# A hybrid decoder layer on one core: matrix factors finished in an earlier pass, retention re-stepped with one root per head, sums of weights written sooner

## The chip, the core and the metric

The kernel runs on one core of a Trainium2 chip. A core has a matrix engine (TensorE, PE in the profile; its weight loads are listed apart as PEld), a vector engine (VectorE, DVE), a scalar engine (ScalarE, ACT), GpSimd (POOL) and a queue processor that here issues nearly all transfers (SyncE, SP). Each engine works through its own list of instructions in order and waits for others by semaphores. The metric is the time of one launch in microseconds (us) of device time.

## The reference, cut to what matters

All is float32: 1024 tokens, model width 2048, 16 heads of width 128, eight of them stick-breaking attention and eight retention.

```python
mod = silu(c) @ w_ada + b_ada
shift, scale, gate = split(mod, 3)
h = rms_norm(x, norm_gain) * (1 + scale) + shift          # 1024 x 2048
proj = h @ w_in                                           # 2048 x 8192
q_sb, k_sb, v_sb, z_sb, q_r, k_r, v_r, z_r = split(proj)  # 1024 columns each
oa = stick_breaking(rms(q_sb), rms(k_sb), v_sb) * silu(z_sb)
o_t = sum_{s<=t} gamma_h^(t-s) (rot(q_t) . rot(k_s)) v_s  # retention, in chunks of 128 tokens:
      # scores within a chunk times a decay mask, plus q times a state carried over the chunks
ob = (o - mean) * rsqrt(var + eps) * gain * silu(z_r)     # mean and variance per head and token
out = x + gate * (concat(oa, ob) @ w_out)
```

## The kernel before, in words

**Precision.** A float32 product is made of three matmuls in the faster fp32r format (`mm3`): each operand is cut into a high half (a rounding copy on ACT) and a low half (operand minus high half, on DVE): high x high, high x low, low x high. `split` does this for a 128x512 tile of weights and takes its buffers from a ring of four.

**The input projection by seven products.** The normalised input, transposed, is a 2x2 arrangement of blocks B11, B12, B21, B22 (eight tiles of 128x512 each, one for each `k` from 0 to 7), the weights of a column pair a 2x2 arrangement A11 to A22. Instead of eight block products the kernel makes seven, in the manner of Strassen and Winograd. Their right-hand factors are B11, B21, B22 and the combinations T1 to T4 (`RIGHT`); for every `k` each must be formed and cut into halves. Their left-hand factors are blocks of weights or sums of them, each cut by `split`. Columns are taken in seven groups: four for stick-breaking (q, k, z, v of two heads each), two for retention's k and v, the last for retention's z. Group 0 goes through the products in the order `ORDER1` = 2 (B21), 7 (T3), 4 (T4), 1 (B11), 6 (T2), 5 (T1), 3 (B22), the others in `ORDER` = 4, 1, 6, 5, 3, 2, 7. An entry is one product for 512 contraction rows and one column block: 12 matmuls of 512 columns (`run_entry`). The left operand of an entry is prepared three entries ahead (`LOOK`).

**Before group 0.** Loads of x, its normalisation, and the modulation from `w_ada` run beside a first projection of seven retention q heads (`start_mm`), done in two passes over the 16 contraction blocks: one for the first 512 tokens, one for the last 512. In the second pass each of the 16 positions has seven heads; after each head, items are taken from two lists. `urgent` holds the whole blocks B21, B12, B22, B11 (scale and shift on ACT) and the halves of B21, `background` the forming of T3 and its halves. After positions 3, 7, 11 and 15 `factors` adds the items of two more `k`. A third list, `late`, holds all of T1, T2, T4, B22 and B11; it is appended to `background` after the second pass and taken off two items at every `tick`, which comes twice an entry, in group 0. Factors of B21, T3, T4 and B11 stay in SBUF until group 0 has used them and are then stored; T1, T2 and B22 are stored at once. Later groups read all factors back through a ring.

**Buffers and queues.** SBUF holds 92 slots of 128x512 float32 that `Slots` hands out, from group 0's 24th entry on by classes: 14 for results, 24 raw weights, 24 ring, 30 attention. A slot given back is used again only once its last reader or its store is done. PE's order is written out by hand; attention runs as generators that `tick` moves on, at most one step a tick, each asking for so many ticks until its next step. `later(n, fn)` puts off a piece of ACT or DVE work by `n` ticks.

**Sums of weights.** In group 0, product 7 needs A11 - A21 and product 3 of every group A12 - A11. Both subtractions are issued in `left`, directly ahead of the split that reads them.

**Stick-breaking.** `prepare(h)` loads q and k, forms the norms' roots, stores a row of key scales and loads it back broadcast (`back`). `sb_attention(h)` begins when that is ready and the head before is far enough: it loads q again and v, splits k, and three ticks later splits q.

**Retention.** `ret_prepare` loads a head's q, k, v and rotates q and k on DVE. `ret_attention` takes nine steps on PE, `gap` ticks apart (3, and 2 from head 5 on; 2 ticks ahead of the first): transpose k of chunks 0 to 3 (`turn_k(0)`), transpose v (`values_in(0)`), states 0 with `turn_k(1)`, `values_in(1)` with scores 0, states 1, values 0, scores 1, values 1, and the turning back of the result (`finish`), whose second half is put off into the next head. One tick after scores DVE multiplies them by the mask (`pT`) and POOL scales q; one tick after states DVE makes the chain of states; one tick after values comes `norm`: four statistics and four aggregates on DVE, a root of ten small instructions (`rsqrt_newton`), and four ACT instructions that read the PSUM bank. The four PSUM banks A0, A1, B, C are used in turn. Retention begins when the last stick-breaking head is done and group 5 has begun; the preparation of head 4 waits for group 6.

**Output projection.** It follows in four column units, the first split in two halves of tokens.

Of the kernel before, what the change touches and what calls it, by code (L numbers as in the profile page):

```python
# [17 lines left out]
P = 128  # L18
S = 1024
D = 2048  # L20
KC = D // P
# [12 lines left out]
RT_GAP2 = 2  # L34
# [18 lines left out]
class Slots:  # L53
# [3 lines left out]
    def __init__(self, pool, n):  # L57
        self.pool, self.of, self.cls, self.need = pool, {}, {}, {}
        self.free = {None: deque(range(n))}

# [17 lines left out]
    def get(self, name, cls=None, dtype=F32, borrow=False):  # L78
        q = self.free.get(cls) or self.free[None]
        if not q and borrow:  # L80
# [18 lines left out]
def layer_kernel(ctx, tc, x, c, w_ada, b_ada, norm_gain, w_in, sb_q_gain, sb_k_gain, ret_norm_gain, w_out,  # L99
# [209 lines left out]
    def left(gi, prod, hh, q):  # L309

        def r(b):
            return raws[gi, q, b, hh]

        def done(b):
            put(raws.pop((gi, q, b, hh)))

        name = f"{gi}_{prod}_{q}_{hh}"
        if q == 4:
            b = "A12" if prod in (2, 3) else "A11"
            w = split(r(b), name)  # L320
            if prod in (5, 3):
                done(b)
            return w
        if prod == 7 and gi == 0:
            t = get(f"S3_{q}_{hh}", "raw", borrow=True)
            nc.vector.tensor_tensor(t, r("A11"), r("A21"), op=ALU.subtract)
            sum_done.add((gi, hh, q, 3))
            w = split(t, name)
            put(t)
            return w  # L330
        if prod == 6:
            while (gi, hh, q, 3) not in sum_done or (gi, hh, q, 1) not in sum_done:
                one_sum(*sums1.popleft())
            while (gi, hh, q, 2) not in sum_done:
                one_sum(*sums2.popleft())
        elif prod == 3:
            nc.vector.tensor_tensor(r("A11"), r("A12"), r("A11"), op=ALU.subtract)
# [7 lines left out]
        return w  # L345

# [106 lines left out]
    def run_entry(j):  # L453
        gi, prod, hh, q = entries[j]
        prepare_entry(j + LOOK)
# [133 lines left out]

    def factors(ks):  # L590
# [15 lines left out]
        def high(n, k):  # L606
            def fn():
                t = facs[n, k, "hi"] = get(f"{n}h_{k}", None, F32R, borrow=True)
                nc.scalar.activation(t, facs[n, k], AF.Copy)  # L609
            return fn  # L610

        def low(n, k):
            def fn():
                src, hi = facs[n, k], facs.pop((n, k, "hi"))
                lo = get(f"{n}l_{k}", None, F32R, borrow=True)
                nc.vector.tensor_tensor(lo, src, hi.bitcast(F32), op=ALU.subtract)
                if n != "B21":
                    put(facs.pop((n, k)))
                if n in FIXED:
                    fixed[n, k] = hi, lo  # L620
                else:
                    store(n, k, hi, lo)
                    put(hi, lo)
            return fn

# [142 lines left out]
    for p in range(KC):  # L768
# [11 lines left out]
        for i, h in enumerate((0, 1, 2, 3, 4, 5, 6) if p < KC - 1 else (3, 4, 5, 6, 0, 1, 2)):  # L780
# [9 lines left out]
            some(urgent, 2)  # L790
            if i in (1, 4, 5, 6):
                some(background, 1)
# [8 lines left out]
    background.extend(late)  # L801
    for j in range(LOOK):
        prepare_entry(j)
# [76 lines left out]
    scales, kss = {}, {}  # L880

    def prepare(h):
# [78 lines left out]
    def sb_attention(h, gap):  # L961
# [8 lines left out]
        q_, k_, v_, qt = {}, {}, {}, []  # L970
        for hf in range(2):
            qt.append(get(f"q_{h}_{hf}", "att"))
            nc.sync.dma_start(qt[hf], proj[f"q{h}"][:, halves(hf)])
# [171 lines left out]
    tables, pending, done_concat = {}, [], set()  # L1145
# [35 lines left out]
    def ret_attention(h, r, gap):  # L1181
# [64 lines left out]
        def values(g):  # L1246
# [10 lines left out]
            def norm():  # L1257
                st6 = sm.tile([P, 4, 6], F32, tag="st6", name=f"st6_{h}_{g}")
                mv = sm.tile([P, 4, 2], F32, tag="mv", name=f"mv_{h}_{g}")
                for j in range(4):  # L1260
                    nc.vector.bn_stats(st6[:, j, :], op[:, j, :])
                for j in range(4):
                    nc.vector.bn_aggr(mv[:, j, :], st6[:, j, :])
                m = sm.tile([P, 4], F32, tag="m4", name=f"m4_{h}_{g}")
                nc.vector.tensor_scalar(m, mv[:, :, 1], EPS, None, op0=ALU.add)
                y = sm.tile([P, 4], F32, tag="y4", name=f"y4_{h}_{g}")
                u = sm.tile([P, 4], F32, tag="u4", name=f"u4_{h}_{g}")
                rsqrt_newton(y, m, u)
                nc.vector.scalar_tensor_tensor(u, mv[:, :, 0], -1.0, y, op0=ALU.mult, op1=ALU.mult)
                for j in range(4):  # L1270
                    nc.scalar.activation(on[:, j * P:(j + 1) * P], op[:, j, :], AF.Identity, scale=y[:, j:j + 1],
                                         bias=u[:, j:j + 1])
            later(1, norm)
# [15 lines left out]
        yield 2  # L1289
# [16 lines left out]
        scores(1)  # L1306
# [3 lines left out]
        yield gap  # L1310
        finish(0)
        pending.append(lambda: finish(1))
        yield gap

    def ret_heads():
        while prog.get(NH - 1, 0) < 99 or phase[0] < 5:
            yield 1
# [5 lines left out]
        yield 16  # L1323
        for h in range(NH):
            r = nxt
            for i, wait in enumerate(ret_attention(h, r, RT_GAP if h < 5 else RT_GAP2)):
# [5 lines left out]
        yield 4  # L1332
        pending.pop()()
# [50 lines left out]
    for i in range(8):  # L1384
        load_at[i] = [(b, i // 4, i % 4) for b in ("A11", "A21")]
        load_at[8 + i] = [("A22", i // 4, i % 4)]
    for i in range(2):
        load_at[16 + i] = [("A11", i, 4)]
    for j in range(len(entries)):
        gi, prod, hh, q = entries[j]  # L1390
        if j == 0 or entries[j - 1][0] != gi:
# [5 lines left out]
            if gi == 5:  # L1397
                start(ret_heads(), 3)
            if gi == 1:
# [151 lines left out]
```

## Time and profile before

| | |
|---|---|
| runs of the kernel before | 2032.77 us median of 3 (2032.35 to 2036.83) |
| the profiled execution | 2034.63 us, its span 2032.9 us |
| PE, share of the span | 95% (1939.3 us) |
| DVE | 61% |
| ACT | 39% |
| POOL | 4% |
| mean granted TensorE clock | 0.985 |
| HBM read, written | 410.04 MB, 75.54 MB |

The profile gives, for each engine, its busy time, what ended its idle times (the releaser), single instructions in order of time, and tables of stretches of time. A name such as `pT<-sp,dm` means that tile pT was written from sp and dm, `L1240` is line 1240 of the kernel, and `x64` counts instructions. Where one helper records every split, rows of different callers have the same line and are told apart by the names of tiles.

### The profile page before, as it was taken

The numbers are of one execution on the slowest core, as the hardware profiler recorded it, in microseconds if no ns is written. First come the engines' busy times: TensorE is split into PE (matmuls) and PEld (weight loads), VectorE is DVE, ScalarE is ACT, GpSimd is POOL, SyncE is SP. The second block draws the span as 40 slices with busy tenths as digits, with TensorE's granted clock in tenths as the row PEclk, the third lists the DMA queues.
The fourth block names the chain that finished last, engine by engine and source line by source line (L and its number), as shares of the span: only waits on it lengthen the run. The fifth ranks groups of instructions, "written<-read, shape, count | busy, mean of one in ns | idle before, by whom it ended". The sixth has DMA issues, their size and how long they took to land.

```text
span 2032.9 us, 28401 instructions
## 1 busy us (share of the span) xinstructions
PE 1939.3 (95%) x9703; PEld 1581.2 (78%) x9703; DVE 1245.0 (61%) x2485; ACT 789.2 (39%) x1481; POOL 78.0 (4%) x278
## 2 busy tenths in 40 slices
PE   5999986999999999999999999999989999999998
PEld 4776764787878877888888888887878778788887
DVE  4645567346767666767686767665866667635122
ACT  5446643224544454445444543333333444211110
POOL 0000000000100010001000010000000000000000
PEclk9999997999999999999999999999999999999999
DMA  9966598798788678867877787989959636745041
GB/s 314 360 223 218 192 314 295 248 342 284 233 269 289 224 238 282 277 230 246 286 269 239 251 277 242 287 263 279 338 176 265 209 120 219 239 128 191 21 151 62
DMA packets 381725, 487.51 MB, mean 240 GB/s; under 512 B 30734, under 2 KB 201864, under 8 KB 381580
## 3 DMA queue, kind: packets, MB, share of 16 engines
q1 hardware_dynamic: 381192, 485.65, 73.0%
q8 instruction: 76, 1.25, 0.3%
q14 instruction: 69, 0.57, 0.1%
q10 hardware_dynamic: 388, 0.04, 0.0%
HBM read 410.04 MB, written 75.54 MB: 239 GB/s over the span
## 4 chain that ended last, share of the span: by engine, by line
PE 77%; DMA 8%; DVE 8%; ACT 3%; issue 2%; SPq 1%; ACTq 0%; DVEq 0%
PE pj L185 14%; PE pj L186 14%; PE pj L187 14%; PE y L185 5%; PE y L186 5%; PE y L187 5%; PE first L185 2%; PE first L186 2%; PE first L187 2%; PE accp L553 1%; DMA q<-pr_q 1%; DVE wl L174 1%; ACT wh L172 1%; PE op L1251 1%; PE oT L187 1%
## 5 line engine op out<-in xcount | busy, mean ns | idle before, releaser
L174 DVE TENSOR_TENSOR wl<-A,wh 128x512 fp32r<-128x512 f32 x392 | 270.3, 691 | 311.6 <-ACT wh L172 285.1
L172 ACT ACTIVATE wh<-A 128x512 fp32r<-128x512 f32 x392 | 246.9, 631 | 390.7 <-PE pj L186 292.2
L185 PE MATMUL y<-wh_o,ch 128*128 128x512 f32 x512 | 201.1, 393 | 2.4 <-ACT ch L1378 2.3
L187 PE MATMUL y<-wh_o,cl 128*128 128x512 f32 x512 | 200.3, 391 | 0.0
L186 PE MATMUL y<-wl_o,ch 128*128 128x512 f32 x512 | 200.0, 391 | 0.0
L174 DVE TENSOR_TENSOR wl_o<-wo,wh_o 128x512 fp32r<-128x512 f32 x80 | 54.9, 690 | 173.9 <-ACT wh_o L172 173.1
L172 ACT ACTIVATE wh_o<-wo 128x512 fp32r<-128x512 f32 x80 | 50.4, 630 | 236.1 <-PE y L187 212.1
L380 DVE TENSOR_TENSOR c<-pj,c 128x512 f32<-128x512 f32 x112 | 75.0, 688 | 75.6 <-PE pj L187 75.4
L377 ACT ACTIVATE c<-pj 128x512 f32<-128x512 f32 x112 | 66.5, 598 | 129.4 <-PE pj L187 109.0
L185 PEld LDWEIGHTS y<-wh_o,ch 128*128 128x128 f32 x512 | 96.6, 189 | 24.5 <-ACT ch L1378 3.1
L187 PEld LDWEIGHTS y<-wh_o,cl 128*128 128x128 f32 x512 | 96.5, 188 | 21.3 <-DVE cl L1379 1.1
L186 PEld LDWEIGHTS y<-wl_o,ch 128*128 128x128 f32 x512 | 96.5, 189 | 19.7
L295 DVE TENSOR_TENSOR A<-A,A 128x512 f32<-128x512 f32 x160 | 108.7, 687 | 1.9
L185 PE MATMUL pj<-T4h,wh 128*128 128x512 f32 x224 | 91.7, 410 | 13.5 <-ACT T4h L609 13.5
L185 PE MATMUL pj<-T3h,wh 128*128 128x512 f32 x224 | 90.3, 403 | 5.1 <-ACT wh L172 5.1
L1030 DVE TENSOR_TENSOR_SCAN om<-om 128x128 f32<-128x128 f32 (+2 forms) x96 | 93.7, 976 | 1.1
L185 PE MATMUL first<-h_hi,wh_first 128*128 128x512 f32 x224 | 92.4, 413 | 1.1 <-ACT h_hi L583 1.1
L185 PE MATMUL pj<-B21h,wh 128*128 128x512 f32 x232 | 93.0, 401 | 0.0
L185 PE MATMUL pj<-B22h,wh 128*128 128x512 f32 x232 | 92.8, 400 | 0.0
L185 PE MATMUL pj<-T1h,wh 128*128 128x512 f32 x232 | 92.6, 399 | 0.0
L187 PE MATMUL pj<-T4h,wl 128*128 128x512 f32 x224 | 89.6, 400 | 3.0 <-DVE wl L174 3.0
L185 PE MATMUL pj<-B11h,wh 128*128 128x512 f32 x232 | 91.4, 394 | 0.0
(236 smaller groups left out, 4620.7 us busy)
## 6 DMA issues: line engine op xcount, KB each, us to landing
A<-in_w_in_dram SPq DMA_DIRECT2D x228, 256.0 KB
ada<-in_w_ada_dram SPq DMA_DIRECT2D x128, 256.0 KB
wo<-in_w_out_dram SPq DMA_DIRECT2D x80, 256.0 KB
gr<-in_w_ada_dram SPq DMA_DIRECT2D x64, 256.0 KB
T2h<-fac_T SPq DMA_DIRECT2D x56, 256.0 KB
T2l<-fac_T SPq DMA_DIRECT2D x56, 256.0 KB
T1h<-fac_T SPq DMA_DIRECT2D x56, 256.0 KB
T1l<-fac_T SPq DMA_DIRECT2D x56, 256.0 KB
```

What stands on the lines that cost most here:

```text
L172: nc.scalar.activation(hi[:, 0:n], src[:, 0:n], AF.Copy)
L174: nc.vector.tensor_tensor(lo[:, 0:n], src[:, 0:n], hi[:, 0:n].bitcast(F32), op=ALU.subtract)
L185: nc.tensor.matmul(o, a_hi, b_hi, start=first, stop=False, skip_group_check=on)
L186: nc.tensor.matmul(o, a_hi, b_lo, start=False, stop=False, skip_group_check=on)
L187: nc.tensor.matmul(o, a_lo, b_hi, start=False, stop=last, skip_group_check=on)
L295: nc.vector.tensor_tensor(r[o], r[a], r[b], op=ALU.add if n == 1 else ALU.subtract)
L377: nc.scalar.activation(t, o, AF.Copy)
L380: nc.vector.tensor_tensor(dst[q, cc], o, dst[q, cc], op=ALU.add)
L553: nc.tensor.matmul(ap_[32 * g:32 * g + 32, :], silu_z[:, j, :], ada[cc, j // 2][:, (j % 2) * 256:(j % 2) * 256 + 256], start=j < 4, stop=j ...
L1030: nc.vector.tensor_tensor_scan(rev, rev, rev, init, op0=ALU.mult, op1=ALU.bypass)
L1251: nc.tensor.matmul(op[:, j, :], pT[:, tk], vb(i), start=True, stop=(i == 0))
```

## The change

Factors: after the second pass's positions 3, 7 and 11, all of T1 to T4 and B22 for two `k` goes into `background` and is taken off within that pass; only the last two `k` (`last`) are left over to group 0, with all halves of B11, which come last of all. The taking off is spread otherwise: one urgent item a head (two at the last position), and background items only while six or fewer urgent ones are left, then one or two a head. `high` and `low` move out of `factors` unchanged.

Sums: `prepare_sum` issues the subtractions two entries ahead of their split; group 0's raw blocks A11, A21, A22 are loaded one entry later. In the last group a slot may be taken from any class (`loose`).

Stick-breaking: q is loaded in `prepare`, behind the broadcast row.

Retention: eight steps, 3 ticks apart for all heads, in another order; statistics of both halves are kept and one root is formed for eight chunks; a copy of the result is taken from PSUM by ACT, and the normalisation later works on that copy in SBUF. Both halves of `finish` are put off into the next head. Its tables and the first head's loads begin before the last stick-breaking head ends.

```diff
     def run_entry(j):
         gi, prod, hh, q = entries[j]
+        prepare_sum(j + LOOK + 2)
         prepare_entry(j + LOOK)
...
+    def prepare_sum(j):
+
+        if j >= len(entries):
+            return
+        gi, prod, hh, q = entries[j]
+        if q < 4 and prod == 3:
+            a = raws[gi, q, "A11", hh]
+            nc.vector.tensor_tensor(a, raws[gi, q, "A12", hh], a, op=ALU.subtract)
+        elif gi == 0 and prod == 7:
+            early_sum[hh, q] = t = get(f"S3_{q}_{hh}", "raw", borrow=True)
+            nc.vector.tensor_tensor(t, raws[gi, q, "A11", hh], raws[gi, q, "A21", hh], op=ALU.subtract)
+            sum_done.add((gi, hh, q, 3))
...
+        last = 7 in ks
         for k in ks:
             urgent.extend(whole(n, k) for n in ("B21", "B12", "B22", "B11"))
             urgent.extend((high("B21", k), low("B21", k)))
-            background.extend((minus("T3", "B22", "B12", k), high("T3", k), low("T3", k)))
-            late.extend((over("T1", "B12", "B11", k), minus("T2", "B22", "T1", k), over("T4", "B21", "T2", k)))
-            order = ("T4", "T1", "T2", "B22", "B11")
-            late.append(high("T4", k))
+        for k in ks:
+            background.extend((minus("T3", "B22", "B12", k), high("T3", k), over("T1", "B12", "B11", k), low("T3", k),
+                               minus("T2", "B22", "T1", k), over("T4", "B21", "T2", k), high("T4", k)))
+            order = ("T4", "T2", "T1", "B22")
             for i, n in enumerate(order):
+                q = late if last and i else background
                 if i + 1 < len(order):
-                    late.append(high(order[i + 1], k))
-                late.append(low(n, k))
+                    (late if last else background).append(high(order[i + 1], k))
+                q.append(low(n, k))
...
-            some(urgent, 2)
-            if i in (1, 4, 5, 6):
-                some(background, 1)
+            if len(urgent) <= 6:
+                some(background, 1 if urgent or i % 4 == 3 else 2)
+            some(urgent, 1 if p < KC - 1 else 2)
...
     background.extend(late)
+    background.append(high("B11", 0))
+    for k in range(8):
+        if k < 7:
+            background.append(high("B11", k + 1))
+        background.append(low("B11", k))
...
                 nc.sync.dma_start(kb[hf], krow[h][:, halves(hf)].broadcast_to([P, HALF]))
+            qs[h] = [get(f"q_{h}_{hf}", "att") for hf in range(2)]
+            for hf in range(2):
+                nc.sync.dma_start(qs[h][hf], proj[f"q{h}"][:, halves(hf)])
...
-            def norm():
+            def stats():
+                nc.scalar.activation(on, op.rearrange("p j n -> p (j n)"), AF.Copy)
...
+            later(1, stats)
+            if g:
+                later(2, roots)
...
+            later(3, lambda: norm(0))
+            later(4, lambda: norm(1))
...
-        yield 2
         turn_k(0)
         yield gap
         values_in(0, vr[0])
-        if pending:
-            pending.pop()()
+        scores(0)
+        yield gap
+        turn_k(1)
         yield gap
         states(0)
-        turn_k(1)
+        scores(1)
         yield gap
         values_in(1, vr[1])
-        scores(0)
-        yield gap
-        states(1)
+        if pending:
+            pending.popleft()()
         yield gap
         values(0)
         yield gap
-        scores(1)
+        states(1)
+        if pending:
+            pending.popleft()()
         yield gap
         values(1)
...
-        while prog.get(NH - 1, 0) < 99 or phase[0] < 5:
+        while prog.get(NH - 1, 0) < 12 or phase[0] < 5:
...
-        load_at[i] = [(b, i // 4, i % 4) for b in ("A11", "A21")]
-        load_at[8 + i] = [("A22", i // 4, i % 4)]
+        load_at[i + 1] = [(b, i // 4, i % 4) for b in ("A11", "A21")]
+        load_at[9 + i] = [("A22", i // 4, i % 4)]
```

More of the change, by code (lines that the diff above doesn't have):

```diff
@@ L33 @@
 RT_GAP = 3
-RT_GAP2 = 2
 NZ = 7
@@ L79, in get @@
         q = self.free.get(cls) or self.free[None]
-        if not q and borrow:
+        if not q and (borrow or self.loose):
             q = max(self.free.values(), key=len)
@@ L324, in left @@
         if prod == 7 and gi == 0:
-            t = get(f"S3_{q}_{hh}", "raw", borrow=True)
-            nc.vector.tensor_tensor(t, r("A11"), r("A21"), op=ALU.subtract)
-            sum_done.add((gi, hh, q, 3))
+            t = early_sum.pop((hh, q))
             w = split(t, name)
@@ L335, in left @@
                 one_sum(*sums2.popleft())
-        elif prod == 3:
-            nc.vector.tensor_tensor(r("A11"), r("A12"), r("A11"), op=ALU.subtract)
         b = {1: "A11", 2: "A12", 3: "A11", 4: "A22", 5: "A22", 6: "A11", 7: "A21"}[prod]
@@ L588, in layer_kernel, with high, fn, low @@
     facs = {}
+    def high(n, k):
+        def fn():
+            t = facs[n, k, "hi"] = get(f"{n}h_{k}", None, F32R, borrow=True)
+            nc.scalar.activation(t, facs[n, k], AF.Copy)
+        return fn
+    def low(n, k):
+        def fn():
+            src, hi = facs[n, k], facs.pop((n, k, "hi"))
+            lo = get(f"{n}l_{k}", None, F32R, borrow=True)
+            nc.vector.tensor_tensor(lo, src, hi.bitcast(F32), op=ALU.subtract)
+            if n != "B21":
+                put(facs.pop((n, k)))
+            if n in FIXED:
+                fixed[n, k] = hi, lo
+            else:
+                store(n, k, hi, lo)
+                put(hi, lo)
+        return fn
     def factors(ks):
@@ L604, in minus @@
             return fn
[L606 to L624, printed above, removed]
         def over(n, a, b, k):
@@ L969, in sb_attention @@
             yield 1
[L970 to L973, printed above, removed]
+        q_, k_, v_ = {}, {}, {}
+        qt = qs.pop(h)
         for hf in range(2):
@@ L1142, in sb_attention @@
         prog[h] = 99
-    tables, pending, done_concat = {}, [], set()
+    tables, pending, done_concat = {}, deque(), set()
     def ret_prepare(h):
@@ L1262, in norm, with roots @@
                 for j in range(4):
[L1263 to L1269, printed above, removed]
-                for j in range(4):
-                    nc.scalar.activation(on[:, j * P:(j + 1) * P], op[:, j, :], AF.Identity, scale=y[:, j:j + 1],
-                                         bias=u[:, j:j + 1])
-            later(1, norm)
+                    nc.vector.bn_aggr(mv[:, 4 * g + j, :], st6[:, j, :])
+            later(1, stats)
+            if g:
+                later(2, roots)
+        mv = sm.tile([P, 8, 2], F32, tag="mv", name=f"mv_{h}")
+        def roots():
+            m = sm.tile([P, 8], F32, tag="m8", name=f"m8_{h}")
+            nc.vector.tensor_scalar(m, mv[:, :, 1], EPS, None, op0=ALU.add)
+            y = sm.tile([P, 8], F32, tag="y8", name=f"y8_{h}")
+            u = sm.tile([P, 8], F32, tag="u8", name=f"u8_{h}")
+            rsqrt_newton(y, m, u)
+            nc.vector.scalar_tensor_tensor(u, mv[:, :, 0], -1.0, y, op0=ALU.mult, op1=ALU.mult)
+            def norm(g):
+                for j in range(4):
+                    i, sl = 4 * g + j, slice(j * P, (j + 1) * P)
+                    nc.scalar.activation(ons[g][:, sl], ons[g][:, sl], AF.Identity, scale=y[:, i:i + 1],
+                                         bias=u[:, i:i + 1])
+            later(3, lambda: norm(0))
+            later(4, lambda: norm(1))
         def finish(g):
@@ L1309, in ret_attention @@
         put(dm_t, *st_t, v[0], v[1])
-        yield gap
-        finish(0)
-        pending.append(lambda: finish(1))
+        pending.extend((lambda: finish(0), lambda: finish(1)))
         yield gap
     def ret_heads():
-        while prog.get(NH - 1, 0) < 99 or phase[0] < 5:
+        while prog.get(NH - 1, 0) < 12 or phase[0] < 5:
             yield 1
@@ L1322, in ret_heads @@
         nxt = ret_prepare(0)
-        yield 16
+        yield 14
+        while prog[NH - 1] < 99:
+            yield 1
         for h in range(NH):
             r = nxt
-            for i, wait in enumerate(ret_attention(h, r, RT_GAP if h < 5 else RT_GAP2)):
+            for i, wait in enumerate(ret_attention(h, r, RT_GAP)):
                 if i == 2 and h < NH - 1:
@@ L1331, in ret_heads @@
                 yield wait
-        yield 4
-        pending.pop()()
+        yield 6
+        pending.popleft()()
+        yield 3
+        pending.popleft()()
         put(*tables.values())
```

8 lines of the change are left out of this document (5 added, 3 removed).

## The prediction

> **What bounds the kernel now.** I read the page's busy shares and clock row first, then what TensorE (PE) waited for, then tables of stretches round the places those waits stand in, and last the order of single instructions there.
>
> ```profile
> span 2032.9 us, 28401 instructions
> PE 1939.3 (95%) x9703; PEld 1581.2 (78%) x9703; DVE 1245.0 (61%) x2485; ACT 789.2 (39%) x1481; POOL 78.0 (4%) x278
> PEclk9999997999999999999999999999999999999999
> ```
>
> PE is busy 95% of the span, so only two things can be won while its matmuls stay as they are: its 93.6 us of idle time, and the time in which it runs at a lower clock (the 7 in the clock row, at about 305 to 356 us). The waits of PE, in total, times and longest:
>
> ```profile
> PE op L1251 <- DVE pT L1240: 20.6, 8, 5.4
> PE pj L185 <- ACT T4h L609: 13.5, 3, 5.7
> PE rows_ps L150 <- DMA x<-in_x_dram: 9.9, 1, 9.9
> PE accp L553 <- DMA ada<-in_w_ada_dram: 9.0, 1, 9.0
> PE zp L185 <- ACT q_0h L180: 7.4, 4, 2.6
> PE pj L185 <- ACT wh L172: 5.1, 3, 2.6
> PE accp L553 <- ACT xT L540: 4.8, 3, 1.6
> PE y L185 <- ACT ch L1378: 2.3, 1, 2.3
> PE tp_A L1050 <- DVE al L1075: 1.5, 8, 0.2
> PE tp_B L1050 <- DVE al L1075: 1.1, 2, 0.5
> ```
>
> The two DMA waits are the first loads, and `y` is the output projection; no edit reaches them. The others lie where the change works. Two tables of stretches give what they cost with the clock (columns: length, PE busy and its instructions, weight loads, DVE, ACT, POOL, granted clock, DMA share, GB/s):
>
> ```profile
> 265.00:341.00 76.00, 52.72 (x182) 36.33 (x181) 56.36 (x90) 33.05 (x61) 0.00 (x0) 0.82 0.91 322
> 341.00:365.00 24.00, 24.00 (x107) 19.90 (x106) 14.61 (x23) 5.69 (x9) 0.00 (x0) 1.00 0.48 165
> 1300.00:1690.00 390.00, 369.39 (x1911) 312.96 (x1910) 256.81 (x664) 142.03 (x265) 21.73 (x16) 0.97 0.75 234
> 270.00:280.00 10.00, 8.03 (x27) 5.81 (x26) 7.75 (x12) 4.46 (x9) 0.00 (x0) 0.83 0.64 209
> 310.00:320.00 10.00, 4.80 (x14) 3.52 (x13) 9.53 (x17) 4.27 (x8) 0.00 (x0) 0.81 1.03 383
> 320.00:330.00 10.00, 2.01 (x3) 0.79 (x3) 8.77 (x15) 3.23 (x6) 0.00 (x0) 0.50 0.73 273
> ```
>
> A wide matmul takes 24.00/107 = 0.224 us when nothing is in its way, so the 182 of 265 to 341 us are worth 40.8 us, and that stretch loses 35.2. DVE is busy 9.5 and 8.8 us of 10 just where PE is empty: group 0 waits for its right-hand factors, which DVE makes late. In 1300 to 1690 us (retention) PE idles 20.6 us and the clock of 0.97 takes 11.7 more: 32.3 us. The clock is lost in the wake of waits: even the 1.97 us idle of 270:280 goes with a granted clock of 0.83.
>
> **The change part by part.** The sum is made against the profiled execution, 2034.63 us with a span of 2032.9; the median of the three runs is 1.86 us below it.
>
> *Factors in the second pass.* In each of three stretches of four blocks of the contraction, two blocks' factors are now finished. Per block that adds three subtractions (T1, T2, T4) and four low halves (T4, T2, T1, B22) on DVE, four high halves on ACT, six stores on SP.
>
> ```profile
> 157.90:186.24 28.34, 26.45 (x173) 19.86 (x172) 16.95 (x30) 17.09 (x29) 0.00 (x0) 1.00 0.79 256
> 186.24:214.54 28.30, 26.40 (x173) 19.86 (x172) 16.95 (x30) 17.09 (x29) 0.00 (x0) 1.00 0.51 161
> 214.54:239.90 25.36, 23.48 (x134) 18.25 (x133) 16.42 (x29) 16.00 (x28) 0.00 (x0) 1.00 0.28 83
> L597 ACT ACTIVATE xT<-xT,shift,mods 128x512 f32<-128x512 f32 x8 | 5.8, 806 | 0.0
> L609 ACT ACTIVATE T3h<-T 128x512 fp32r<-128x512 f32 x2 | 1.3, 627 | 0.5 <-DVE T L603 0.5
> L616 DVE TENSOR_TENSOR T3l<-T,T3h 128x512 fp32r<-128x512 f32 x2 | 1.4, 684 | 0.0
> ```
>
> DVE: 14 x 0.684 = 9.6, on 16.95: 26.5 of 28.3 us. ACT: 8 x 0.627 = 5.0, on 17.09: 22.1. Both fit, DVE with 1.8 us to spare; PE hides them. If order makes half of DVE's 11.4 free us useless, 3.9 us a stretch shows, 12 in all: the upper end. The lower end is -4.8: the waits of `accp` for `xT` come behind four whole-block activations in one go (the row of 8, 5.8 us), and the new loop issues one urgent item a head, not two, and no background item while over six urgent ones are left. I take -3, near the lower end, because the row that shows a wait here blames the burst. DMA: 36 stores x 262 KB = 9.4 MB; the free shares of the three rows (0.21, 0.49, 0.72) are 38 us, at 256/0.79 = 324 GB/s worth 12.3 MB.
>
> *Group 0.* It keeps only the last two blocks' factors and all B11 halves (56 items, 28 each on DVE and ACT). Popped four per group of 12 matmuls (2.7 us), they are out in 14 groups (38 us). DVE then carries 28 + 14 splits + 8 sums, 50 x 0.69 = 34.5 of 38 us, and T4 (wanted at group 18) is ready long before. The sums are written two groups ahead of their split, so ACT doesn't queue behind a sum that DVE has only just been given. What is late next: raw weights. A11 and A21 are loaded a group later and wanted two groups sooner, so the lead shrinks from seven groups to four (10.9 us). The last pair follows 7 spills, 14 raw blocks, 16 stores of B21 and about 4 late stores; with itself 43 transfers, 11.3 MB, 29 us at the 383 GB/s of 310:320, wanted at 33 us. DVE waits of some us in its order are likely; the splits stand three groups (8 us) ahead and take most. I leave 4 of the 35.2 us: -31. Bounds: all of it, -35; and -20 if the raw blocks come 15 us late in sum (near the 13.5 that T4 cost).
>
> By the Trainium skill, "DMA: Bandwidth & Descriptors", section "Where 436 GB/s comes from", loads from HBM bind at about 358 GB/s per core; the 383 GB/s row (loads and stores mixed) stands above it. By the page those 43 transfers would take 31.5 us, and an estimated 2 us more would be left in group 0.
>
> *Stick-breaking's q.* It is loaded in the preparation, behind the broadcast key row, not at the head's start. The chain of waits shows the load and the split in a row; the rows of waits and of clock give the price:
>
> ```profile
> 578.20 6.60 DMA q<-pr_q
> 585.49 0.70 DVE q_0l L181
> PE zp L187 <- DVE q_0l L181: 0.9, 4, 0.2
> 508.00:610.00 102.00, 98.68 (x502) 81.04 (x501) 68.59 (x127) 49.74 (x98) 8.75 (x43) 0.98 0.78 251
> ```
>
> 7.4 + 0.9, and 2% of 102 us for the clock: 10.3 at most. It holds two more of 30 attention buffers for most of a head; that can make a load wait for a buffer, hence -9 (bounds -10.3 and 0).
>
> *Sums of weights in the other groups (L337).* ACT waits for these, PE seldom:
>
> ```profile
>   ACT wh L172: 74.0, 35
> ```
>
> The same DVE work, two groups sooner. What PE loses there is 1.5 + 1.1 us behind `al`. Bounds -2.6 and +2 (a sum that waits for A12's load blocks DVE sooner, 2 groups being less than the raw ring's lead); I take -1.5.
>
> *Retention.* Rows in order of time, around one of its stalls:
>
> ```profile
> 1486.13 0.17 DVE L1265 TENSOR_SCALAR m<-mv 128x4 f32<-128x4 f32 x1
> 1489.45 0.16 DVE L1269 SCALAR_TENSOR_TENSOR u<-mv,y 128x4 f32<-128x4 f32 x1
> 1489.65 1.51 ACT L1271 ACTIVATE on<-op,u,y 128x128 f32<-128x128 f32 x4 [10.31 <-DVE u L1269]
> 1493.04 0.68 DVE L1164 TENSOR_TENSOR sw_k<-sw_k,sin 128x512 f32<-128x512 f32 x1
> 1495.57 0.68 DVE L1240 TENSOR_TENSOR pT<-sp,dm 128x512 f32<-128x512 f32 x1
> 1496.31 0.79 PE L1251 MATMUL op<-rv,pT 128*128 128x128 f32 x2 [5.38 <-DVE pT L1240]
> ```
>
> The chain of small root instructions takes DVE from 1486.1 to 1489.6; ACT, in order, stands 10.31 us before the normalisation and its next splits follow late, so DVE reaches the masks at 1495.6 and PE waits 5.38. Three edits cut it. Scores now stand four steps ahead of their values (before two and one); one root per head replaces two (about 3.5 us of DVE less a head); and the normalisation is put three and four ticks after the root, reading a copy in SBUF, so neither ACT nor the PSUM bank waits for the root. Added: 16 copies of PSUM on ACT, 16 x 0.6 = 10 us, off the path (ACT 142 of 390 us). The new tight place is the second state chain, one step (three ticks, over 4 us of PE work) ahead of the second values: three small DVE instructions, but behind a rotation (three times 0.68). No row shows it late; the nearest is the wait that goes, 20.6 us in 8 times, and that stood behind root and normalisation too. A rotation in the way costs 2.0 us; in two of eight heads, with half a us of clock each, that is 5: I keep 5 of 32.3 and take -27. Bounds: -32, and 0 if the wait only changes its name. Head 0 starts some 14 ticks earlier (its tables and rotations run beside stick-breaking's tail); head 3 then waits for the next group's phase, while PE has the projection to do: nothing.
>
> The Trainium skill, "TensorE: Matmul & The Clock Gate", Part 1, has the clock fall to half after an idle window of about 3.4 us. The 1.97 us wait of 270:280 with clock 0.83 disagrees; by the page my remaining short waits would cost no clock, and the sum would be some 3 us lower.
>
> **Sum.** -3 - 31 - 9 - 1.5 - 27 = -71.5, from 2034.6 to 1963.1; as a median of runs, 1.86 less: about 1961 us.
>
> **The rivals.**
> 1. *Every gap closes.* 4.8 + 35.2 + 10.3 + 2.6 + 32.3 = 85 us: 1948. For it: no matmul is added. Against: DVE stays at 26.5 of 28.3 us.
> 2. *DVE bounds the second pass.* +12 instead of -3: 1976. For it: 94% in that sum. Against: `make_h` and the splits stand two blocks ahead.
> 3. *Group 0 stays short of raw weights.* -20 instead of -31: 1972.
> 4. *Retention's wait only moves* to the state chain: 27 less: 1988. Against: the chain's DVE work is not what made DVE late; root and normalisation did.
> 5. *SP's queue holds the second pass; slower.* The stores now stand in SP's queue ahead of the weight loads, and the second of a pair is issued only when its low half is written:
>
> ```profile
> 160.31 5.35 SPq L495 DMA_DIRECT2D ada<-in_w_ada_dram  x8
> 276.72 0.34 SPq L350 DMA_DIRECT2D fac_T<-T1h  x1
> 279.29 0.34 SPq L351 DMA_DIRECT2D fac_T<-T1l  x1
> 270.22 0.69 DVE L616 TENSOR_TENSOR B22l<-xT,B22h 128x512 fp32r<-128x512 f32 x1 [5.29 <-DMA fac_T<-T1h]
> ```
>
> At 0.67 us an issue, six loads and three stores are 6.0 of 7.07 us a block, 12.8 us spare over 12 blocks. With 18 pairs that each hold SP for X, 18X - 12.8 shows. X = 2.2 (the two rows of T1) gives 27 us: 1988. It turns slower from X = 4.7; at 5.3, the one long hold in the rows, 83 us: 2044. Against: the low half stands within 2 us of its high half while DVE keeps up, and buffers are fewer in use than before (seven per finished block, not eight).
> 6. *Short waits cost no clock.* Of my remainders about 3 us are clock (1 in retention, 2 in group 0); without them 1958. Against: the 0.83 of 270:280. The clock-gate page's rule would have it so.
>
> **How the numbers follow.** Forecast 0.40, every gap 0.13, DVE 0.13, raw weights 0.12, retention's move 0.09, SP 0.07 (0.03 of it slower), no clock cost 0.06. The likeliest is 1961, its own range 1953 to 1970. From 1946 to 1990 no more than about 0.1 is left out. About 0.2%, 4 us, is what a measurement of this kernel can tell from no change: faster 0.95, same 0.01, slower 0.04.
>
> **What would show it.** In the profile after: no `op <- pT` among PE's waits, and the 1300 to 1690 stretch's clock near 1.00; no `pj <- T4h`, and group 0's part from T3 to T4's end some 35 us shorter; `zp <- q_0h` gone; DVE over 24 of 28 us in the second pass with `accp <- xT` under 2 us. Wrong would be: the second pass's stretch of four blocks longer than 28.3 us; new PE waits for `state`, `wh_first` or raw `A` in place of the old ones; low clock still in the stretches round group 0.

## The result, and the profile after

The changed kernel takes 1972.32 us (median of four runs, 1969.98 to 1973.15) against 2032.56 for the kernel before in the runs beside it (2032.29 to 2036.83). The ratio is 0.9697, with a 95% interval of 0.968 to 0.9714: some 61 us faster. The forecast was 1961 (1946 to 1990). The profiled execution took 1972.75 us, with a span of 1971.0.

The first lines of the changed kernel's page: span, busy time of each engine, granted clock in forty slices.

```profile
span 1971.0 us, 28290 instructions
PE 1918.2 (97%) x9703; PEld 1573.3 (80%) x9703; DVE 1222.5 (62%) x2389; ACT 800.0 (41%) x1497; POOL 81.1 (4%) x278
PEclk9999989999999999999999999999999999999999
```

PE's idle time fell from 93.6 to 52.8 us. Its busy time fell by 21.1 us although the same 9703 matmuls run: that is the clock (a mean of 0.985 before and 0.995 after; in the clock row a 7 at 305 to 356 us before, now an 8 earlier, at 246 to 296).

What PE waited for after the change (total, times, longest):

```profile
PE rows_ps L150 <- DMA x<-in_x_dram: 9.8, 1, 9.8
PE accp L565 <- DMA ada<-in_w_ada_dram: 8.7, 1, 8.7
PE accp L565 <- ACT xT L552: 5.0, 2, 2.5
PE pj L185 <- ACT zt L775: 4.4, 1, 4.4
PE tp_B L1070 <- DVE om L1047: 3.4, 4, 1.5
PE op L1273 <- DVE state L1247: 3.2, 1, 3.2
PE xtp L545 <- DVE shift L588: 2.4, 2, 1.2
```

The three rows that headed the old list behind the first loads are gone: `op <- pT` (20.6), `pj <- T4h` (13.5) and `zp <- q_0h` (7.4). The two rows of the first loads stand as they were. New are `pj <- zt` and `op <- state`; `tp_B <- om` (in stick-breaking) and `xtp <- shift` have grown, each from 0.9 us; `accp <- xT` did not shrink.

Where the time went shows when both executions are cut at the same matmuls: the end of the second pass (first matmul of group 0, product B21), the first of T3, the first of group 1, the first of group 5. Tables of stretches, columns as in the prediction. The kernel before:

```profile
239.90:268.70 28.80, 28.80 (x136) 24.11 (x135) 13.71 (x22) 18.34 (x33) 0.00 (x0) 1.00 1.07 345
268.70:452.50 183.80, 159.34 (x650) 124.09 (x649) 104.79 (x162) 60.76 (x106) 0.00 (x0) 0.93 0.87 294
300.10:347.40 47.30, 29.16 (x98) 20.32 (x97) 39.28 (x63) 22.02 (x42) 0.00 (x0) 0.75 0.94 345
452.50:1250.80 798.30, 784.27 (x3945) 645.46 (x3944) 557.71 (x1029) 366.41 (x711) 55.56 (x256) 1.00 0.79 260
```

The changed kernel:

```profile
157.70:190.00 32.30, 28.29 (x174) 20.43 (x173) 25.58 (x44) 20.55 (x37) 0.00 (x0) 0.95 0.64 222
190.00:220.70 30.70, 26.67 (x173) 19.78 (x172) 24.80 (x43) 20.56 (x37) 0.00 (x0) 1.00 0.83 280
220.70:248.40 27.70, 23.29 (x134) 18.16 (x132) 22.82 (x41) 19.03 (x34) 0.00 (x0) 0.96 0.76 231
248.40:281.60 33.20, 32.50 (x134) 26.34 (x135) 21.98 (x37) 20.93 (x38) 0.00 (x0) 0.88 1.04 339
281.60:303.40 21.80, 21.80 (x98) 18.05 (x97) 16.84 (x28) 14.05 (x26) 0.00 (x0) 1.00 1.00 341
303.40:325.10 21.70, 21.70 (x97) 18.00 (x96) 13.39 (x20) 6.03 (x10) 0.00 (x0) 1.00 1.06 384
325.10:431.10 106.00, 104.15 (x458) 85.44 (x457) 42.98 (x65) 26.46 (x43) 0.00 (x0) 1.00 0.83 268
431.10:1216.60 785.50, 779.43 (x3945) 644.92 (x3944) 555.49 (x1029) 366.54 (x711) 57.90 (x256) 1.00 0.80 265
1216.60:1608.30 391.70, 388.06 (x2045) 329.71 (x2043) 263.79 (x596) 157.03 (x284) 22.48 (x16) 1.00 0.82 256
1300.00:1640.00 340.00, 336.79 (x1762) 286.13 (x1761) 218.00 (x514) 145.95 (x265) 18.19 (x13) 0.99 0.81 252
```

Read against each other:

| Stretch | before | after | difference | forecast |
|---|---|---|---|---|
| second pass (its end: 239.9, now 248.4), and group 0's first product (28.8, now 33.2) | | | +8.5 and +4.4 = +12.9 | -3 |
| T3 of group 0 to group 1 | 183.8 | 149.5 | -34.3 | -31 |
| groups 1 to 4 (q, sums) | 798.3 | 785.5 | -12.8 | -10.5 |
| group 5 to the end (retention, output) | 782.1 | 754.4 | -27.7 | -27 |

The sum is -61.9, the difference of the spans. Three of four terms came out within 3.3 us. The second pass did not: its stretches of four blocks take 32.3, 30.7 and 27.7 us where they took 28.34, 28.30 and 25.36, and the clock is low in group 0's first product.

Why, the order of single instructions shows. ACT in the second pass, after the change (start, length, engine, line, operation; in brackets the idle time ahead and what ended it):

```profile
178.99 0.63 ACT L605 ACTIVATE T3h<-T 128x512 fp32r<-128x512 f32 x1 [3.46 <-DVE T L635]
181.71 0.63 ACT L605 ACTIVATE T4h<-xT 128x512 fp32r<-128x512 f32 x1 [2.09 <-DVE xT L642]
183.70 0.57 ACT L552 ACTIVATE xT<-xtp 128x512 f32<-128x512 f32 x1
...
241.35 0.64 ACT L605 ACTIVATE T3h<-T 128x512 fp32r<-128x512 f32 x1 [3.89 <-DVE T L635]
244.07 0.63 ACT L605 ACTIVATE T4h<-xT 128x512 fp32r<-128x512 f32 x1 [2.08 <-DVE xT L642]
247.73 3.49 ACT L775 ACTIVATE zt<-first 128x512 f32<-128x512 f32 x7
```

PE, a moment behind each:

```profile
184.32 3.33 PE L565 MATMUL accp<-ada,silu_z 128*32 128x256 f32 x32 [2.50 <-ACT xT L552]
248.36 0.79 PE L185 MATMUL pj<-B21h,wh 128*128 128x512 f32 x1 [4.41 <-ACT zt L775]
```

`T3h` and `T4h`, the high halves, stand on ACT directly behind the subtractions on DVE that make their input, and ACT takes its list in order. It stands 3.46 and 2.09 us for them; what it has behind them, the copies `xT` and `zt` that empty PSUM, comes late; and PE waits for those. ACT's waits in 157.7 to 282 us, changed kernel:

```profile
ACT T4h L605 <- DVE xT L642: 15.8, 8, 2.2
ACT T3h L605 <- DVE T L635: 14.3, 5, 3.9
```

That is 30.1 us of standing on an engine whose copies PE needs. DVE itself was busy 25.58 of 32.3 us: not full, but not in step with ACT.

### The profile page after: what moved, and what is told of

It reads as the page before. It is cut to its first block, busy times and chain, and to the rows that moved or that the text cites. A ratio compares the mean times of both kernels' runs of the same rounds, so it can differ in the third digit from the quotient of the medians.

```text
span 1971.0 us, 28290 instructions
## 1 busy us (share of the span) xinstructions
PE 1918.2 (97%) x9703; PEld 1573.3 (80%) x9703; DVE 1222.5 (62%) x2389; ACT 800.0 (41%) x1497; POOL 81.1 (4%) x278
## 4 chain that ended last, share of the span: by engine, by line
PE 85%; DVE 6%; DMA 5%; ACT 2%; issue 1%; SPq 0%; DVEq 0%; ACTq 0%
PE pj L185 17%; PE pj L187 17%; PE pj L186 16%; PE y L185 5%; PE y L187 5%; PE y L186 5%; PE first L185 2%; PE first L186 2%; PE first L187 2%; PE accp L565 2%; DVE wl L174 1%; PE tp_B L1070 1%; PE zp L185 1%; PE zp L187 1%; PE zp L186 1%
## 5 line engine op out<-in xcount | busy, mean ns | idle before, releaser
L187 PEld LDWEIGHTS y<-wh_o,cl 128*128 128x128 f32 x512 | 96.1, 188 | 21.1 <-DVE cl L1413 1.1
L1050 DVE TENSOR_TENSOR_SCAN om<-om 128x128 f32<-128x128 f32 (+2 forms) x96 | 93.6, 974 | 1.1
L187 PE MATMUL pj<-B21h,wl 128*128 128x512 f32 x232 | 92.7, 399 | 0.7 <-DVE wl L174 0.7
L186 PE MATMUL pj<-B21l,wh 128*128 128x512 f32 x232 | 92.1, 397 | 0.0
L187 PE MATMUL pj<-T1h,wl 128*128 128x512 f32 x232 | 90.7, 391 | 0.0
```

What stands on the lines that cost most here:

```text
L186: nc.tensor.matmul(o, a_hi, b_lo, start=False, stop=False, skip_group_check=on)
L187: nc.tensor.matmul(o, a_lo, b_hi, start=False, stop=last, skip_group_check=on)
L1050: nc.vector.tensor_tensor_scan(rev, rev, rev, init, op0=ALU.mult, op1=ALU.bypass)
```

## The experiments

Each kernel was timed beside the kernel before on the same chip. Ratios are to that kernel; differences to the changed kernel are differences of ratios times 2033 us, each uncertain by some 5 us (two intervals of about 0.0017 either way).

### One part undone at a time

**Old factors.** The second pass and `late` as before, with group 0's sums and loads as before (its early sums need slots that the old factors hold); the rest of the change stays.

```diff
-        last = 7 in ks
...
+            background.extend((minus("T3", "B22", "B12", k), high("T3", k), low("T3", k)))
+            late.extend((over("T1", "B12", "B11", k), minus("T2", "B22", "T1", k), over("T4", "B21", "T2", k)))
...
+            some(urgent, 2)
+            if i in (1, 4, 5, 6):
+                some(background, 1)
```

> The changed kernel with the factors formed and taken off as before, and group 0's sums and loads as before (SBUF has no room for early sums beside the old factors); retention, q and the other groups' sums stay changed. Theory (the stages add): start to the first product of group 1 took 452.5 us before and 431.1 after, so undoing costs those 21 us: 1993 us, group 0 starting near 240 us again and T4 taking 47 us. Rival (stages don't add; the later parts gain from group 0's state): 2000 or more, or under 1985.

Measured: 1995.71 us, ratio 0.9809 [0.9793, 0.9826], so 23 us more than with the change. PE waits again for `T4h`:

```profile
PE pj L185 <- ACT T4h L603: 13.4, 3, 5.6
```

Group 0 starts at 241.1 us and T3 at 269.9, 11.7 earlier than after the change; from T3 to group 1 it takes 185.3 us, 35.8 more. The new factors are worth some 35 us in group 0 and cost some 12 ahead of T3: the table's first two lines again. Group 0's early sums, which went with them, are part of the 35; undone alone (below) they come to 2.8 us there.

**Old retention.** The old nine steps, one root and one normalisation for each half head, straight from PSUM; the rest of the change stays.

```diff
-            later(1, stats)
-            if g:
-                later(2, roots)
...
-            later(3, lambda: norm(0))
-            later(4, lambda: norm(1))
...
+        scores(1)
         yield gap
         values(1)
```

> The changed kernel with retention's steps, roots and start as before. Theory (the stages add): from group 5's first product to the end the change won 28 us, so 2000 us, with PE's op <- pT waits back at about 20 us. Rival (the waits at values belonged to where retention stood in group 5 and 6, which has shifted): under 1985, with op <- pT under 8 us.

Measured: 1995.28 us, 0.9803 [0.9785, 0.9821], 22 us more, where the theory had 28 and the rival under 13; by the two traces, from group 5's first matmul to the end it takes 780.1 us against 754.4. The old wait is back, eight times, as the theory had it:

```profile
PE op L1272 <- DVE pT L1261: 19.7, 8, 5.4
```

**New order of steps, old root and normalisation.** This one divides the retention term.

```diff
+            def norm():
...
-            later(1, stats)
-            if g:
-                later(2, roots)
...
+                rsqrt_newton(y, m, u)
...
+                    nc.scalar.activation(on[:, j * P:(j + 1) * P], op[:, j, :], AF.Identity, scale=y[:, j:j + 1],
+                                         bias=u[:, j:j + 1])
+            later(1, norm)
```

> The changed kernel with its eight steps in the new order, but the normalisation as before: a root per half, one tick after values, ACT reading the PSUM bank. Theory (root and normalisation are what makes DVE late; the order only changes which of its products is the last): op <- pT gone, op <- state 10 to 20 us, about 1988 us. Rival (the order alone pays): op <- state stays at 3 us, 1975 or less.

Measured: 1987.2 us, 0.977 [0.9755, 0.9785]. PE's waits from 1215 us on, and one of ACT's in 1215 to 1615 us:

```profile
PE op L1273 <- DVE state L1247: 9.5, 3, 7.5
PE y L185 <- ACT ga L875: 5.0, 1, 5.0
PE y L185 <- ACT ch L1401: 2.3, 1, 2.3
ACT on L1291 <- DVE u L1289: 48.3, 9, 6.5
```

The order alone removes `op <- pT`, and the wait moves to the state chain, as the prediction's fourth rival had it: 9.5 us in three times, one of 7.5. ACT stands 48.3 us for the roots again, and `ga`, a copy for the output projection, comes late behind the last of them: PE waits 5.0 us for it. Of the 22 us, order (with its even gaps and the earlier start) gives some 7; the root per head and the later normalisation from SBUF give some 15 (by the traces from group 5 on, 9.4 and 16.3). Which of these two parts of the normalisation gives how much was not tried.

**Old q.** Its load moves from `prepare` back into `sb_attention`.

```diff
-            for hf in range(2):
-                nc.sync.dma_start(qs[h][hf], proj[f"q{h}"][:, halves(hf)])
...
+            nc.sync.dma_start(qt[hf], proj[f"q{h}"][:, halves(hf)])
```

> The changed kernel with q loaded at the head's start again. Theory: 10 of the 13 us won in the four stick-breaking groups are q's: 1982 us, four zp <- q_0h waits of 2 us each back, and a low clock after some. Rival: the early sums keep DVE and ACT free enough that the late q no longer shows: 1974 or less.

Measured: 1976.28 us (1970.06 to 1978.99), 0.9707 [0.9683, 0.973]: 2 us more, which can't be told from none; it lies between what theory and rival said. The wait returns at less than half its old size:

```profile
PE zp L185 <- ACT q_0h L180: 3.3, 4, 1.7
```

**Old sums.** `prepare_sum` goes, both subtractions go back into `left`, group 0's loads to their old places.

```diff
+            nc.vector.tensor_tensor(t, r("A11"), r("A21"), op=ALU.subtract)
...
-        prepare_sum(j + LOOK + 2)
...
-        load_at[i + 1] = [(b, i // 4, i % 4) for b in ("A11", "A21")]
+        load_at[i] = [(b, i // 4, i % 4) for b in ("A11", "A21")]
```

> The changed kernel with the sums issued directly ahead of their split and group 0's loads as before. Theory: they cost PE only what stands behind al and om in the stick-breaking groups: 2 to 4 us, 1974 to 1976. Rival: they carry a good part of group 0's gain (there ACT waited 11.5 us for S): 1985 or more, with pj <- wh waits of 5 us in T3.

Measured: 1982.3 us, 0.974 [0.9722, 0.9759], 9 us more (7.6 by the spans), between what the theory and its rival said. It is spread out: 2.8 us more in group 0 (248.2 to 433.7 us), 1.9 in groups 1 to 4, 3.1 from group 5 on, and no new PE wait over 2.1 us carries it. Only the part in group 0 is clear of what executions differ by: groups 1 to 4 take 783.1 to 788.5 us in the eleven kernels here that have the changed kernel's instructions there, and 787.4 in this one. One wait that the early sums bring goes again, after 3.4 us in four times with them:

```profile
PE tp_B L1073 <- DVE om L1050: 0.9, 1, 0.9
```

With q undone, groups 1 to 4 take 791.3 us (in the slowest of that kernel's executions), 2.8 above the highest of the eleven and 5.8 above the changed kernel's 785.5. Neither part undone alone brings back the 12.8 us that both together made.

### The second pass: what costs the 13 us

The end of this pass differs from execution to execution: the changed kernel and the four above that leave its second pass alone start group 0 between 246.2 and 249.1 us. Theories: bursts (up to 13 items fall into one block's seven heads), the last two blocks' items just ahead of `zt`, the order of the items, or the sum of DVE's work.

**Even.** The 28 background items of a stretch are spread over its heads, one a head, two at four of them.

```diff
-            if len(urgent) <= 6:
-                some(background, 1 if urgent or i % 4 == 3 else 2)
+            n = p % 4 * 7 + i
+            if p >= 4 and n >= 4:
+                some(background, 2 if n % 4 == 0 and 12 <= n <= 24 else 1)
```

> The changed kernel with the same 28 background items per stretch of the second pass, spread evenly (one a head from a stretch's fifth head on, two at four heads) instead of up to 13 in one block's seven heads. Theory (bursts: DVE is busy 25.6 of the 32.3 us, ACT stands 30 us in all before T3 and T4 and xT's copy behind it): the stretches go from 32.3, 30.7 and 27.7 us to 29 or less each, accp <- xT under 2 us; about 1964 us. Rival (DVE's sum with its waits for high halves is too long at any pace): the stretches keep 30 us and more, 1970 to 1975.

Measured: 1968.76 us, 0.968 [0.9662, 0.9698], some 3.5 us less than the change, less than half of the 8 expected and within the uncertainty; group 0 starts at 246.6 us, inside the spread above. `accp <- xT` falls to 0.6 us, and ACT still stands 23.9 us for DVE's subtractions.

**Stop early.** No background item in the last two blocks of the second pass.

```diff
-            if len(urgent) <= 6:
+            if len(urgent) <= 6 and p < KC - 2:
```

> The changed kernel with no background items taken off in the second pass's last two blocks; what is left (18 items) goes to group 0. Theory: the 4.4 us wait of group 0's first product for zt and the low clock after it come from ACT standing behind DVE's T3 and T4 there; both go, 8 us less, 1964 us. Rival: group 0 cannot take 18 more items (DVE 42 of its first 38 us), and the time comes back as pj <- wh or pj <- T4h waits: 1970 or more.

Measured: 1969.73 us, 0.9687 [0.9672, 0.9703], 2 us less, which can't be told from none. `pj <- zt` is gone and group 0 starts 3.9 us earlier (244.5), but what was left undone comes in group 0 ahead of its splits:

```profile
PE pj L185 <- ACT wh L172: 3.4, 2, 2.9
```

Group 1 starts at 430.5 us, 0.6 earlier: given back, as the rival had it. **Even and stop early** together:

```diff
+            if 4 <= p < KC - 2 and n >= 4:
```

> Both edits of y1_even and y2_stop_early. Theory: the second pass ends near 240 us as before the change, nothing else moves: 1958 us. Rival (they repair the same loss): 1964.

Measured: 1971.43 us, 0.9693 [0.9678, 0.9707], no gain; `pj <- wh` is 4.4 us there, and PE waits once 4.9 us for DVE's copy out of the modulation's bank (`xtp <- acc`). The theory that the items' place in the pass is the whole cause fell.

**Late highs.** The pacing stays as changed; a `k`'s items take another order: all subtractions first, each high half six or more items behind its subtraction (in the last two `k`, of which only T3 and T4 are finished here, four and two items behind).

```diff
+            seq = [minus("T3", "B22", "B12", k), over("T1", "B12", "B11", k), high("B22", k), minus("T2", "B22", "T1", k),
+                   over("T4", "B21", "T2", k), low("B22", k), high("T3", k), high("T1", k), low("T3", k), high("T2", k),
+                   low("T1", k), high("T4", k), low("T2", k), low("T4", k)]
```

> The changed kernel with that order of items and its own bursts (up to 13 items a block). Theory O: most of the gain comes with the order alone: 1965. Rival L: 1970 to 1973, as the changed kernel.

Measured: 1969.52 us, 0.9682 [0.9666, 0.9697], as much as "even" gives, again within the uncertainty and nearer to rival L than to theory O; group 0 starts at 244.0 us. **Even and late highs**, both edits:

```diff
+            if p >= 4 and n >= 4:
+                some(background, 2 if n % 4 == 0 and 12 <= n <= 24 else 1)
...
+            seq = [minus("T3", "B22", "B12", k), over("T1", "B12", "B11", k), high("B22", k), minus("T2", "B22", "T1", k),
```

> y1_even with a block's 14 items in another order: all subtractions first, each high half six or more items behind the subtraction that it reads, so that ACT need not stand behind DVE. Theory O: ACT's waits for T and xT go from 30 us to under 5, mod and accp <- xT and pj <- zt with them; 1962 to 1964 us. Rival L (DVE's load): stretches stay near 29.5 us, 1967 to 1970.

Measured: 1963.77 us (1963.71 to 1965.1), 0.9653 [0.9638, 0.9669], the fastest, and its interval lies below the changed kernel's. Stretches of this kernel, cut as above:

```profile
157.70:240.70 83.00, 77.50 (x482) 58.51 (x480) 70.91 (x125) 60.25 (x106) 0.00 (x0) 1.00 0.81 271
240.70:273.90 33.20, 30.70 (x134) 25.26 (x135) 24.02 (x40) 21.21 (x38) 0.00 (x0) 0.95 1.04 340
273.90:422.50 148.60, 147.52 (x650) 121.58 (x650) 72.24 (x110) 46.49 (x79) 0.00 (x0) 1.00 0.89 297
```

The second pass ends at 240.7 us, 0.8 behind the kernel before and 5.5 ahead of the spread above, with 70.91 of 83 us on DVE. ACT's waits for T and T4, 157.7 to 282 us:

```profile
ACT T4h L605 <- DVE xT L642: 3.0, 3, 1.5
ACT T3h L605 <- DVE T L635: 2.5, 1, 2.5
```

30.1 us have become 5.5 ("even" alone left 23.9, late highs alone 14.1). So it was the standing behind DVE, with the bursts, and not DVE's sum: the same work fits (125 instructions of DVE here, 127 in the changed kernel's second pass). ACT now stands 8.8 us for loads of weights instead, and PE waits for none of them. What is left is 4.4 us in the first product of group 0, with one 2.5 us wait for a split's low half and the clock at 0.95.

**Even, with POOL taking the low halves of T1, T2 and B22**, to take DVE's sum down:

```diff
-            nc.vector.tensor_tensor(lo, src, hi.bitcast(F32), op=ALU.subtract)
+            (nc.vector if n in FIXED else nc.gpsimd).tensor_tensor(lo, src, hi.bitcast(F32), op=ALU.subtract)
```

> y1_even with the low halves of T1, T2 and B22 made by POOL instead of DVE (six of the 20 factor instructions a stretch; the last two blocks' too, in group 0). Theory L (what is left of the second pass's loss is DVE's load): DVE loses 6 x 0.6 = 3.6 us a stretch, xtp <- acc, xtp <- shift and pj <- zt fall under 2 us in all, about 1961 us. Rival O (what is left is ACT standing in order behind DVE's subtractions): 1967 to 1970. A third (POOL and DVE hold each other up): over 1970, with DVE instructions over 1 us.

Measured: 1974.93 us, 0.9708 [0.9691, 0.9725], 6 us more than "even". Groups of instructions in 157.7 to 245 us:

```profile
L612 DVE TENSOR_TENSOR T4l<-xT,T4h 128x512 fp32r<-128x512 f32 x5 | 8.9, 1781 | 0.0
L612 POOL TENSOR_TENSOR B22l<-xT,B22h 128x512 fp32r<-128x512 f32 x5 | 8.6, 1729 | 0.0
L612 DVE TENSOR_TENSOR T3l<-T,T3h 128x512 fp32r<-128x512 f32 x6 | 4.1, 691 | 0.0
```

`T4l`, which runs on DVE beside POOL's, takes 1781 ns where `T3l`, the same instruction with none beside it, takes 691, and where `T4l` itself takes 683 in "even". What POOL took off DVE, DVE lost in longer instructions: it is busy 76.43 us in 157.7 to 247 us here, with 108 instructions, and 74.30 us in 157.7 to 248 us of "even", with 130. The third theory had it so.

**Even, late highs, and the modulation's PSUM bank emptied by ACT** in column blocks 9 to 15 (the last is 15), the shifts added by ACT too:

```diff
-        nc.vector.tensor_copy(acc[:, 0:256], ap_)
+        if cc >= 9:
+            nc.scalar.activation(acc[:, 0:256], ap_, AF.Copy)
...
+            for s in range(2):
+                nc.scalar.activation(shift[:, k0 + s:k0 + s + 1], mod[:, s:s + 1], AF.Identity,
+                                     bias=shift_b[:, k0 + s:k0 + s + 1])
```

> z2_even_late_highs with PSUM bank C of the second pass (modulation sums and their columns) emptied by ACT instead of DVE, so that no wait of PE there depends on DVE's queue. Theory O: xtp <- shift and acc go too, 2 to 5 us less than z2: 1959 to 1961. Rival L: ACT is not late, so this takes away DVE's lateness wherever it shows; the loss moves to h_lo or wl, no gain over z2.

Measured: 1966.14 us (1964.38 to 1969.22), 0.9665 [0.9648, 0.9682]. Group 0 starts 1.6 us earlier (239.1), and in total nothing is gained, as rival L had it. The best kernel remains "even and late highs".

## Why the prediction was right, and where it was off

**Bound and direction: right.** PE's idle time and its clock were the only things to win, and both were won where the prediction said, but for the second pass. Three of the signs that it named for being wrong came all the same: stretches of four blocks longer than 28.3 us, a wait for `state`, and a low clock round group 0.

**The second pass (-3 forecast, +12.9 measured): the term that was mis-sized**, by 15.9 us; the other terms took 6.3 of it back. The instruction count and durations held (14 more on DVE, 8 on ACT in a stretch of four blocks). The step that failed is "I take -3, near the lower end, because the row that shows a wait here blames the burst", which let a gentler urgent burst count and the new background burst not. The value was that of the second rival (+12), but not by its mechanism: that rival has DVE bound by its sum, and 70.91 of 83 us in the best kernel shows that the sum fits. The prediction's own reason for its upper end ("If order makes half of DVE's 11.4 free us useless") was the right one. What was missed is that an item's two engines couple: each high half directly behind its subtraction hands DVE's queue to ACT, and ACT carries the copies that free PSUM. Of the 12.9 us, new order and pacing together return about 8 in the second pass; of group 0's first product, 4.4 us stay.

**Group 0 (-31; -34.3): right.** T4's wait is gone, and from T3's first matmul to T4's last it takes 43.5 us (281.6 to 325.1) against 78.7 (268.7 to 347.4), 35.2 less. The raw weights, named as what is late next, were not late: PE's wait for the splits made from them, 5.1 us for `wh` before, is gone from its list, and for `wl` 0.7 us are left.

**q and the sums (-10.5 together; -12.8): right in sum, the split not borne out.** q undone costs 2 us in all, not 9. Sums undone cost 9, not 1.5, but that run undoes group 0's sums as well, which belong to the term above (2.8 us). With the sums early, the wait for a late q is 3.3 us, not the 7.4 that the step priced; that the early sums are what shortens it is argued, not tried. The step for the sums priced 1.5 + 1.1 us behind `al`: the 1.5 stay, the 1.1 go, and `om` takes 2.5 more, so PE's waits don't show a gain there. Which waits the sums' 9 us are made of is not shown.

**Retention (-27; -27.7): right**, with the remainder where it was put: `op <- state`, 3.2 us once, and a clock of 0.99 in 1300 to 1640 us. The run with the order alone shows that the fourth rival was near: without the new root and normalisation the wait would have moved to the state chain.

**SP's queue (fifth rival).** The holds that it named are there: SP stands 18.8 us for `T2h` and 18.7 for `T2l` in the changed kernel's second pass, six times each:

```profile
SPq L361 <- ACT T2h L605: 18.8, 6, 6.6
SPq L362 <- DVE T2l L612: 18.7, 6, 3.6
```

That is 37.5 us against the 12.8 that the rival counted as spare; by its sum 24.7 us would have shown. Yet no PE wait for a weight load came of it: the holds fall on six pairs, and the weights must have been loaded further ahead than the rival's sum allows for (how far was not tried). The rival was wrong in what its holds cost, not in the holds.

**The clock (sixth rival): it lost.** Short waits still cost clock; the last section has the rows.

## What to carry to other kernels

Whether work fits beside an engine is not read from that engine's busy sum alone: follow each moved item to the next engine in its chain, and ask what stands behind it in that engine's list. Put the consumer on the other engine some instructions behind its producer, and spread such pairs evenly; both edits together were worth some 8 us here with the same instructions. When a chain is cut at one point (retention's masks), the next tight place in the same chain is where the wait goes, unless what made the engine late goes too.

## What the runs showed of the hardware

**A low clock lasts beyond the wait that brings it.** Stretches of the changed kernel:

```profile
180.00:190.00 10.00, 7.50 (x50) 4.51 (x49) 8.09 (x14) 4.77 (x10) 0.00 (x0) 0.83 0.60 210
248.40:258.40 10.00, 9.30 (x25) 6.88 (x26) 5.01 (x9) 8.85 (x16) 0.00 (x0) 0.60 1.02 379
```

A wait of 2.50 us at 181.8 to 184.3 goes with a clock of 0.83 over the ten us round it. Behind the 4.41 us wait for `zt`, PE is busy 9.30 of the next 10 us, and the clock is 0.60 all the same, worth 8 us at half. Stretches cut where the clock changes show the two dips and what stands ahead of them:

```profile
181.29:184.70 3.41, 0.91 (x11) 0.38 (x13) 2.37 (x5) 2.99 (x7) 0.00 (x0) 1.00 0.53 195
184.70:188.11 3.41, 3.41 (x33) 1.59 (x22) 3.41 (x6) 1.74 (x4) 0.00 (x0) 0.50 0.27 101
249.56:252.97 3.41, 2.71 (x7) 2.15 (x7) 2.56 (x5) 3.41 (x7) 0.00 (x0) 0.50 1.03 383
252.97:256.38 3.41, 3.41 (x9) 2.64 (x8) 1.20 (x2) 3.41 (x7) 0.00 (x0) 0.50 1.02 381
```

The clock falls at 184.70 us for one step of 3.41 us and at 246.15 for three; the two falls are 18 such steps apart. The step ahead of the first fall holds 0.91 us of PE work, the one ahead of the second 1.22. The second dip lasts because PE still waits in its first step, and 0.70 us (for a split's low half) in its second; the first step that PE fills ends it. Each cut on such a grid, the fourteen traces of this case show the same: every fall follows a step with at most 1.75 us of PE work, and every return ends one with at least 2.84.

The Trainium skill, "TensorE: Matmul & The Clock Gate", Part 1, has the clock fall after an idle window of about 3.4 us and return after one busy window of that length, the windows running freely. The traces agree in the windows and in the return. They disagree in the fall: by the page a wait of 2.5 us would have cost nothing, and here a step about half empty was enough.

**Two-input work on DVE runs longer beside POOL's.** `T4l` takes 683 ns in "even" and 1781 beside POOL. The Trainium skill, "SBUF — State Buffer", section "Who interferes with whom", says that a DVE instruction with two SBUF inputs contends with a GpSimd instruction that reads SBUF; the trace agrees, and gives the price.
